# A decoder trunk on one core: the mixers' own products in float32r, and the modulation sums in other stages

## The chip, the cores and the metric

The kernel runs on one core of one Trainium2 chip. The metric is the device time of one execution in microseconds. Three runs of the kernel before gave 998.33, 993.95 and 998.08 us, a median of 998.08 us.

## The reference

Two residual layers work on 256 positions of 1024 channels. Each layer has three sub-layers: a half-step SwiGLU (inner width 2816), a mixer, and another half-step SwiGLU. Each is preceded by an RMSNorm with a shift and a scale, and followed by a gate; shift, scale and gate come from a conditioning vector c through a 1024 x 18432 product, two halves of which are the two layers' 9 x 1024.

```python
def modnorm(x, g, shift, scale):
    return rmsnorm(x, g) * (1 + scale[:, None, :]) + shift[:, None, :]
def swiglu(h, w_gate, w_up, w_down):
    return (jax.nn.silu(h @ w_gate) * (h @ w_up)) @ w_down
...
# even mixer: p = h @ w_in, split in u, q, k, v; the output is concat(pool(u), diff_attention(q, k, v)) @ w_out
#   pool, group g of 4, window w = 2, 4, 8, 16:
#     pooled = trailing mean over min(pos + 1, w) positions - u;  y = (pooled @ w_group[g]) * scale
#   diff_attention, 4 heads with two halves of 64 channels:
#     s = causal(q . k / 8);  p = softmax(s);  a = p[0] - lam * p[1];  o = rmsnorm(a @ v)
# odd mixer: mLSTM in two chunks of 128 positions; its decay matrices need rows of running maxima, one per head
```

All of it is in float32, the positions lie along the free dimension, the channels along the 128 partitions.

## The kernel before, in words

The work is one stream of 2560 weight tiles of 128 x 128, called units, in a fixed order: gate and up of the first feed-forward (352 units), down (176), the even mixer's input projection (128) and output projection (64), the second feed-forward (528), then layer 1 in the same way with an input projection of 192. A unit (`mm3`, L338) is three float32r matmuls with 256 columns, with weight and activation each split into a high part rounded to float32r and the rest: wh x rh (L341), wl x rh (L342), wh x rl (L343).

Sixteen units are a chunk, one DMA of 1 MiB on SP's queue (L294) into a ring of five buffers `raw`. Half a chunk, eight units, is split by ScalarE (high half `wh`, L299) and VectorE (low half `wl`, L300), with four buffers for each; `split_to` runs two halves ahead of the unit that is issued (`look`). The modulation product runs beside this on VectorE: a modulation chunk, also 1 MiB on the same queue and in the same ring (L249), holds two columns, each of which is one multiply and sum of 128 x 1024 (L267, in `mod_sums`) with c. `MOD_POINTS` (L121) says how many of the 72 modulation chunks are read before which weight chunk, by straight lines between points; they are loaded in front of the weights of that chunk and summed behind its second low half. The columns are needed by `need_mod` in the sequence norm, gate, norm, and so on.

The order of the work around the stream is written out by hand. A piece of a mixer is a generator, a lane, which yields the number of units after which it continues; `tick` runs the lanes due at each unit, so their instructions stand between the matmuls of the stream in each engine's queue. If something is asked for before its lane has reached it, `run_until` steps all lanes at once.

At the start of a sub-layer the statistics of the norm are not yet there. The first pairs of blocks (`NEARLY`, 5) therefore multiply with the unnormalised x (`xh`, `xl`, 258 columns with the shift) and are scaled with `rext` on the way out of PSUM; meanwhile `stats_lane` makes the statistics (unit 15 and 22) and from then on normalises one of eight parts of x every four units (`norm_x`, L442, three operations on VectorE, ScalarE, VectorE), which the later blocks read as `xs`.

In the even mixer `head(h)` computes scores: for each half a product of an identity with a constant mask over 384 columns (L660), then q . k in fp32 with 64 rows, 128 and 256 columns (L662, L664), maximum on VectorE (L671), exponential on ScalarE (L675). `pool_group` multiplies u with w_pool (L730) and the result with a band matrix of 128 x 384 (L735 to L737), all in fp32. In the odd mixer `gates` broadcasts four rows of maxima to all partitions by an fp32 product (L842). The output projection takes its inner tiles in the order `EVEN_OUT_K`, for the first blocks all but the last ones first (`sweep`).

Of the kernel before, what the change touches and what calls it, by code (L numbers as in the profile page):

```python
# [38 lines left out]
EVEN_OUT_K = (4, 5, 6, 3, 2, 7, 1, 0)  # L39
# [3 lines left out]
NEARLY = 5  # L43
# [48 lines left out]
def weight_units():  # L92

    units = []
    for l in range(DEPTH):
        for s in range(2):
# [24 lines left out]
MOD_POINTS = ((8, 8), (41, 32), (72, 44), (104, 56), (124, 68), (145, 72))  # L121
# [15 lines left out]
def trunk_kernel(ctx: ExitStack, tc: tile.TileContext, xT, crow, pack, pack2, wst, mst, outT):  # L137
# [7 lines left out]
    hid = ctx.enter_context(tc.tile_pool(name="hid", bufs=46))  # L145
# [34 lines left out]
    masks3 = const.tile([P, 3 * P], F32R, name="masks3")  # L180
# [3 lines left out]
    band = const.tile([P, len(WINDOWS), 3 * P], F32, name="band")  # L184
# [23 lines left out]
    def constants():  # L208
        m3 = tmp.tile([P, 2, 3 * P], F32, tag="sc", name="m3")[:, 0, :]
        nc.gpsimd.memset(m3, 0.0)  # L210
        for i in (0, 2):
            nc.gpsimd.affine_select(out=m3[:, i * P:(i + 1) * P], in_=m3[:, i * P:(i + 1) * P], pattern=[[-1, P]],
                                    compare_op=ALU.is_ge, fill=NEG, base=0, channel_multiplier=1)
        nc.gpsimd.tensor_copy(masks3, m3)
# [7 lines left out]
        for g, w in enumerate(WINDOWS):  # L222
            nc.gpsimd.memset(band[:, g, :], 1.0 / w)
            for t in range(w - 1):
                nc.gpsimd.memset(band[:, g, t:t + 1], 1.0 / (t + 1))
            for lo, n in ((0, T), (T, P)):
                m = band[:, g, lo:lo + n]
                nc.gpsimd.affine_select(out=m, in_=m, pattern=[[1, n]], compare_op=ALU.is_ge, fill=0.0,
                                        base=0, channel_multiplier=-1)
                nc.gpsimd.affine_select(out=m, in_=m, pattern=[[-1, n]], compare_op=ALU.is_ge, fill=0.0,  # L230
                                        base=w - 1, channel_multiplier=1)
                nc.gpsimd.tensor_tensor(out=m[:, 0:P], in0=m[:, 0:P], in1=ident, op=ALU.subtract)
        nc.sync.dma_start(pk2, pack2)
        nc.gpsimd.tensor_copy(wgh, pcol("w_gates", 0, 64))
        nc.gpsimd.tensor_tensor(out=wgl, in0=pcol("w_gates", 0, 64), in1=wgh.bitcast(F32), op=ALU.subtract)

# [187 lines left out]
    def stats_lane(wait, key, then=None):  # L424
# [60 lines left out]
    def swiglu(f, hs, gate, bias_g, up, bias_u):  # L485

        sg = tmp.tile([P, T], F32, tag="sg", name=nm("sg"))
# [148 lines left out]
    def even_mixer(l, nxt):  # L636
# [17 lines left out]
        def head(h):  # L654
            yield 8
            q, kk = parts.pop(("q", h)), parts.pop(("k", h))
            pp = [one(), one()]
            for c in range(2):
                rows = slice(64 * c, 64 * c + 64)
                nc.tensor.matmul(pp[c][:, 0:3 * P], lhsT=identr, rhs=masks3, start=True, stop=False,  # L660
                                 skip_group_check=True)
                nc.tensor.matmul(pp[c][:, 0:P], lhsT=q[rows, 0:P], rhs=kk[rows, 0:P], start=False, stop=True,  # L662
                                 skip_group_check=True)
                nc.tensor.matmul(pp[c][:, P:3 * P], lhsT=q[rows, P:T], rhs=kk[rows, 0:T], start=False, stop=True,  # L664
                                 skip_group_check=True)
# [3 lines left out]
            for i in range(2):  # L669
                for c in range(2):  # L670
                    nc.vector.tensor_reduce(out=mx[:, i, c:c + 1], in_=pp[c][:, cols[i]], axis=AX.X, op=ALU.max)  # L671
            nc.vector.tensor_scalar(out=nb, in0=mx, scalar1=-0.125, scalar2=None, op0=ALU.mult)
            for i in range(2):
                for c in range(2):
                    nc.scalar.activation(sc[:, c, cols[i]], pp[c][:, cols[i]], AF.Exp, bias=nb[:, i, c:c + 1],  # L675
# [48 lines left out]
        def pool_group(g, src, bias):  # L724
            u = keep(src, bias)
            yield 16
            pz = one()
# [305 lines left out]
```

## Time and profile before

| | before |
|---|---|
| median of three runs | 998.08 us |
| profiled execution | 998.09 us |
| its span | 996.4 us |
| TensorE matmuls | 973.5 us busy, 98% |
| VectorE | 758.1 us, 76% |
| ScalarE | 528.0 us, 53% |
| GpSimd | 217.9 us, 22% |
| moved by DMA | 247.18 MB, 248 GB/s on average |

The span runs from the first to the last instruction of the profiled execution. Busy times of different engines overlap. A matmul's record is longer than the distance to the next one, because matmuls are pipelined, so the distance of two starts is its price in a stream. An fp32 matmul shows as two records. The stages of the first layer begin at about 17.7 (gate and up), 150.3 (down), 212.5 (input projection), 273.6 (output projection) and 301.7 us (second feed-forward); the odd mixer's input projection runs from 679.3 to 772.6 us.

### The profile page before, as it was taken

Reading aid. Unit: us, or ns where it says so; the run is one execution under the profiler, and the core shown is the slowest. Engines: PE = TensorE matmul, PEld = TensorE weight load, DVE = VectorE, ACT = ScalarE, POOL = GpSimd, SP = SyncE. Lnnn points to the kernel's source line nnn. Section 1 sums busy time; section 2 is a strip of 40 time slices with the busy share of each in tenths; the row PEclk is TensorE's granted clock in tenths of the full one; section 3 lists DMA queues with packets and bytes.
Section 4 is the critical chain, followed back from the end, with each engine's and each line's share of the span. In section 5 each row is a group of like instructions: output and inputs, shape, how many; then the busy total and the mean of one; then the engine's idle time right before and its main releaser. Section 6 shows DMA issues by size and latency. Waiting matters only on the chain.

```text
span 996.4 us, 19641 instructions
## 1 busy us (share of the span) xinstructions
PE 973.5 (98%) x8032; PEld 958.8 (96%) x8032; DVE 758.1 (76%) x1201; ACT 528.0 (53%) x872; POOL 217.9 (22%) x223
## 2 busy tenths in 40 slices
PE   7999999999999999999999999999999999999996
PEld 6899999999999999999999999999899999999996
DVE  5979998989879876777798676788867988555452
ACT  3475544448766544444465444445767655444441
POOL 4953220110112322211122222001010113222011
PEclk9999999999999999999999999999999999999998
DMA  9978888875846766766758766676565746565521
GB/s 341 317 295 318 328 329 319 341 284 206 298 155 246 271 245 254 277 252 235 290 182 291 288 245 248 269 293 258 200 223 185 280 171 244 205 229 175 187 105 43
DMA packets 36093, 247.18 MB, mean 248 GB/s; under 512 B 4001, under 2 KB 4385, under 8 KB 7458
## 3 DMA queue, kind: packets, MB, share of 16 engines
q1 hardware_dynamic: 35856, 245.81, 66.7%
q8 instruction: 63, 1.03, 0.4%
q14 instruction: 28, 0.23, 0.1%
q10 hardware_dynamic: 146, 0.11, 0.0%
HBM read 244.86 MB, written 1.05 MB: 247 GB/s over the span
## 4 chain that ended last, share of the span: by engine, by line
PE 82%; DVE 9%; ACT 3%; issue 3%; POOL 1%; DVEq 0%; ACTq 0%; POOLq 0%
PE one L343 26%; PE one L341 26%; PE one L342 26%; DVE wl L300 3%; DVE rawm L267 3%; ACT wh L299 1%; DVE xs L447 1%; POOL hr L401 1%; DVE xn L445 1%; PE one L418 0%; DVE xl L587 0%; DVE t L512 0%; DVE h L490 0%; ACT L488 0%; PE one L842 0%
## 5 line engine op out<-in xcount | busy, mean ns | idle before, releaser
L300 DVE TENSOR_TENSOR wl<-raww,wh 128x1024 fp32r<-128x1024 f32 x320 | 395.5, 1239 | 162.4 <-ACT wh L299 161.1
L299 ACT ACTIVATE wh<-raww 128x1024 fp32r<-128x1024 f32 x320 | 337.2, 1056 | 226.7 <-PE one L343 197.3
L341 PE MATMUL one<-xs,wh 128*128 128x256 f32 x976 | 275.3, 282 | 0.0
L342 PE MATMUL one<-xs,wl 128*128 128x256 f32 x976 | 272.9, 280 | 1.0 <-DVE wl L300 1.0
L343 PE MATMUL one<-xs,wh 128*128 128x256 f32 x976 | 273.1, 280 | 0.0
L341 PE MATMUL one<-hid,wh 128*128 128x256 f32 x832 | 233.7, 281 | 0.2 <-ACT hid L601 0.2
L343 PE MATMUL one<-hid,wh 128*128 128x256 f32 x832 | 233.7, 281 | 0.0
L342 PE MATMUL one<-hid,wl 128*128 128x256 f32 x832 | 233.3, 280 | 0.0
L342 PE MATMUL one<-xh,wl 128*128 128x258 f32 (+1 forms) x752 | 207.5, 285 | 3.2 <-DVE wl L300 2.9
L341 PE MATMUL one<-xh,wh 128*128 128x258 f32 (+1 forms) x752 | 208.1, 287 | 1.8 <-ACT xh L585 1.8
L343 PE MATMUL one<-xl,wh 128*128 128x258 f32 (+1 forms) x752 | 204.6, 283 | 0.0
L493 POOL TENSOR_TENSOR hid<-h,hid 128x256 fp32r<-128x256 f32 x88 | 123.3, 1402 | 340.1 <-ACT hid L492 340.1
L342 PEld LDWEIGHTS one<-xs,wl 128*128 128x128 f32 x976 | 183.6, 188 | 1.4 <-DVE wl L300 1.2
L341 PEld LDWEIGHTS one<-xs,wh 128*128 128x128 f32 x976 | 183.0, 187 | 1.2 <-issue 1.0
L343 PEld LDWEIGHTS one<-xs,wh 128*128 128x128 f32 x976 | 183.1, 188 | 0.0
L341 PEld LDWEIGHTS one<-hid,wh 128*128 128x128 f32 x832 | 156.8, 188 | 0.4 <-ACT hid L601 0.4
L343 PEld LDWEIGHTS one<-hid,wh 128*128 128x128 f32 x832 | 156.6, 188 | 0.2 <-DVE hid L602 0.2
L342 PEld LDWEIGHTS one<-hid,wl 128*128 128x128 f32 x832 | 156.7, 188 | 0.0
L267 DVE CUSTOM_DVE_ANT_0 rawm<-rawm,cact,pk 128x1024 f32<-128x1024 f32 x112 | 150.5, 1371 | 0.0
L342 PEld LDWEIGHTS one<-xh,wl 128*128 128x128 f32 x752 | 140.6, 191 | 5.4 <-DVE wl L300 5.2
L341 PEld LDWEIGHTS one<-xh,wh 128*128 128x128 f32 x752 | 140.3, 191 | 4.1 <-ACT xh L585 2.3
L343 PEld LDWEIGHTS one<-xl,wh 128*128 128x128 f32 x752 | 138.8, 189 | 0.2 <-DVE xl L587 0.2
(222 smaller groups left out, 727.0 us busy)
## 6 DMA issues: line engine op xcount, KB each, us to landing
raww<-wst SPq DMA_DIRECT2D x152, 1024.0 KB, 4.8
rawm<-mst SPq DMA_DIRECT2D x71, 1024.0 KB, 4.9
raww<-wst SPq DMA_DIRECT2D x16, 512.0 KB, 6.4
xa<-xT SPq DMA_DIRECT2D x2, 512.0 KB, 4.7
rawm<-mst SPq DMA_DIRECT2D x2, 512.0 KB, 7.4
outT<-fin SPq DMA_DIRECT2D x3, 256.0 KB, 2.8
pk<-pack SPq DMA_DIRECT2D x1, 416.0 KB, 6.9
outT<-fin SPq DMA_DIRECT2D x2, 128.0 KB, 2.3
```

What stands on the lines that cost most here:

```text
L267: nc.vector.tensor_tensor_reduce(out=ri, in0=ri, in1=cact, scale=factor, scalar=first, op0=ALU.mult, op1=ALU.add, accum_out=modc[n // KT][ ...
L299: nc.scalar.activation(whs[i], src, AF.Copy)
L300: ins = nc.vector.tensor_tensor(out=wls[i], in0=src, in1=whs[i].bitcast(F32), op=ALU.subtract)
L341: nc.tensor.matmul(out, lhsT=wh, rhs=rh, start=start, stop=False, skip_group_check=skip)
L342: nc.tensor.matmul(out, lhsT=wl, rhs=rh, start=False, stop=False, skip_group_check=skip)
L343: nc.tensor.matmul(out, lhsT=wh, rhs=rl, start=False, stop=stop, skip_group_check=skip)
L401: nc.gpsimd.tensor_tensor(out=r, in0=v, in1=mhalf[:, 0:width], op=ALU.pow)
L445: nc.vector.scalar_tensor_tensor(out=xn, in0=x[k], scalar=a, in1=r, op0=ALU.mult, op1=ALU.mult)
L447: nc.vector.scalar_tensor_tensor(out=to[1], in0=xn, scalar=b, in1=to[0].bitcast(F32), op0=ALU.add, op1=ALU.subtract)
L493: nc.gpsimd.tensor_tensor(out=hl[:, 0:T], in0=h, in1=hh[:, 0:T].bitcast(F32), op=ALU.subtract)
```

## The change

The even mixer's q and k are kept as high and low float32r parts, and the scores are three float32r products per block of scores, with the two row halves in alternation; the mask is added on VectorE in one operation with the maximum, and the exponential reads the result from SBUF. Pooling is done on VectorE by shifted sums, in front of w_pool, which is then three float32r products. The row broadcast of the odd mixer uses two float32r products in place of one fp32 product. `MOD_POINTS` has other points. x is normalised every 7 units, with six early pairs. The even output projection has another order of inner tiles and another sweep. The lanes' yields of `head` and `pool_group` are other ones.

```diff
-EVEN_OUT_K = (4, 5, 6, 3, 2, 7, 1, 0)
+EVEN_OUT_K = (4, 5, 3, 6, 2, 1, 0, 7)
+PAD = 16
-NEARLY = 5
+NEARLY = 6
-                units += [(("out_even", l // 2), k, n) for n, k in sweep(range(KT), EVEN_OUT_K, 3, 2)]
+                units += [(("out_even", l // 2), k, n) for n, k in sweep(range(KT), EVEN_OUT_K, 4, 4)]
-MOD_POINTS = ((8, 8), (41, 32), (72, 44), (104, 56), (124, 68), (145, 72))
+MOD_POINTS = ((8, 8), (20, 18), (33, 31), (45, 32), (78, 47), (111, 68), (145, 72))
-    hid = ctx.enter_context(tc.tile_pool(name="hid", bufs=46))
+    hid = ctx.enter_context(tc.tile_pool(name="hid", bufs=44))
...
         for k in range(KT):
-            yield 4
+            yield 7
             norm_x(k, rext[:, 0:T], A_cols[key][:, k:k + 1], shift[:, k:k + 1], xs[k])
...
         def head(h):
-            yield 8
+            yield 10
             q, kk = parts.pop(("q", h)), parts.pop(("k", h))
             pp = [one(), one()]
-            for c in range(2):
-                rows = slice(64 * c, 64 * c + 64)
-                nc.tensor.matmul(pp[c][:, 0:3 * P], lhsT=identr, rhs=masks3, start=True, stop=False,
-                                 skip_group_check=True)
-                nc.tensor.matmul(pp[c][:, 0:P], lhsT=q[rows, 0:P], rhs=kk[rows, 0:P], start=False, stop=True,
-                                 skip_group_check=True)
-                nc.tensor.matmul(pp[c][:, P:3 * P], lhsT=q[rows, P:T], rhs=kk[rows, 0:T], start=False, stop=True,
-                                 skip_group_check=True)
+            for to, qs, ks in ((slice(0, P), slice(0, P), slice(0, P)), (slice(P, 3 * P), slice(P, T), slice(0, T))):
+                for j, (a, b) in enumerate(((0, 0), (1, 0), (0, 1))):
+                    for c in range(2):
+                        rows = slice(64 * c, 64 * c + 64)
+                        nc.tensor.matmul(pp[c][:, to], lhsT=q[a][rows, qs], rhs=kk[b][rows, ks], start=j == 0,
+                                         stop=j == 2, skip_group_check=True)
...
-                    nc.vector.tensor_reduce(out=mx[:, i, c:c + 1], in_=pp[c][:, cols[i]], axis=AX.X, op=ALU.max)
+                    nc.vector.tensor_tensor_reduce(
+                        out=sc[:, c, cols[i]], in0=pp[c][:, cols[i]], in1=masks3[:, cols[i]], scale=1.0, scalar=NEG,
+                        op0=ALU.add, op1=ALU.max, accum_out=mx[:, i, c:c + 1])
...
         def pool_group(g, src, bias):
-            u = keep(src, bias)
-            yield 16
...
+            w = WINDOWS[g]
+            u = tmp.tile([P, PAD + T], F32, tag="sg", name=nm("pu"))
+            nc.vector.memset(u[:, 0:PAD], 0.0)
+            nc.scalar.activation(u[:, PAD:PAD + T], src, AF.Identity, bias=bias)
+            s, d = u, 1
+            while d < w:
+                n = tmp.tile([P, PAD + T], F32, tag="ps", name=nm("ps"))
+                lo = 2 * d - 1
+                nc.vector.tensor_tensor(out=n[:, lo:PAD + T], in0=s[:, lo:PAD + T], in1=s[:, lo - d:PAD + T - d],
+                                        op=ALU.add)
+                s, d = n, 2 * d
...
+            yield 22
             ps = one()
-            nc.tensor.matmul(ps[:, 0:P], lhsT=z[:, 0:P], rhs=band[:, g, 0:P], start=True, stop=True)
-            nc.tensor.matmul(ps[:, P:T], lhsT=z[:, 0:P], rhs=band[:, g, P:T], start=True, stop=False)
-            nc.tensor.matmul(ps[:, P:T], lhsT=z[:, P:T], rhs=band[:, g, T:3 * P], start=False, stop=True)
+            sl = slice(g * P, (g + 1) * P)
+            for j, (a, b) in enumerate(((wph, zh), (wpl, zh), (wph, zl))):
+                nc.tensor.matmul(ps[:, 0:T], lhsT=a[:, sl], rhs=b[:, 0:T], start=j == 0, stop=j == 2)
...
+            ph, pl = slot(F32R), slot(F32R)
+            nc.scalar.activation(ph[:, 0:T], src, AF.Identity, bias=bias)
+            nc.vector.scalar_tensor_tensor(out=pl[:, 0:T], in0=src, scalar=bias, in1=ph[:, 0:T].bitcast(F32),
+                                           op0=ALU.add, op1=ALU.subtract)
+            parts[blk] = (ph, pl)
...
             for h in range(NH):
                 pb4 = one()
-                nc.tensor.matmul(pb4[:, 0:T], lhsT=ident[0:4, h:h + 1].broadcast_to([4, P]), rhs=mr,
-                                 start=True, stop=True)
+                for j in range(2):
+                    nc.tensor.matmul(pb4[:, 0:T], lhsT=identr[0:4, h:h + 1].broadcast_to([4, P]), rhs=mrs[j],
+                                     start=j == 0, stop=j == 1)
```

In the part of `pool_group` left out, VectorE forms the mean minus the token (one operation over all positions, two short ones for the first w - 1), and z is split into a high part on ScalarE and a low part on VectorE. The `band` constants, 4 x 128 x 384, are no longer made on GpSimd; w_pool is split there into two float32r tiles.

## Rows read from the trace of the kernel before

**Rows 1.** The page, busy us, share of the span and instructions of each engine.
```profile
PE 973.5 (98%) x8032; PEld 958.8 (96%) x8032; DVE 758.1 (76%) x1201; ACT 528.0 (53%) x872; POOL 217.9 (22%) x223
```

**Rows 2.** Windows: length, busy us by engine, then clock, DMA share, GB/s.
```profile
74.00:150.30 76.30, 76.30 (x647) 76.30 (x646) 70.73 (x98) 39.91 (x60) 22.13 (x18) 1.00 0.85 324
150.30:212.50 62.20, 62.20 (x530) 62.20 (x529) 54.63 (x82) 29.22 (x38) 6.17 (x7) 1.00 0.84 320
160.00:170.00 10.00, 10.00 (x87) 10.00 (x86) 9.47 (x19) 4.75 (x8) 0.87 (x1) 1.00 0.96 381
212.50:273.60 61.10, 60.53 (x486) 57.07 (x485) 55.34 (x118) 44.60 (x114) 6.48 (x5) 1.00 0.71 257
```

**Rows 3.** Timeline of TensorE: start, us, instruction, count; 24 matmuls between the two starts.
```profile
688.53 0.28 PE L772 MATMUL one<-xh,wgh 128*8 128x258 f32 x1
...
691.37 0.28 PE L341 MATMUL one<-xh,wh 128*128 128x258 f32 x1
```

**Rows 4.** Timeline of TensorE: the score groups of two heads.
```profile
233.45 0.52 PE L660 MATMUL one<-masks,identr 128*128 128x384 f32 x2
233.90 0.50 PE L662 MATMUL one<-hid,hid 64*128 64x128 f32 x4
234.22 0.61 PE L664 MATMUL one<-hid,hid 64*128 64x256 f32 x4
234.76 0.39 PE L341 MATMUL one<-xh,wh 128*128 128x258 f32 x1
...
257.08 0.34 PE L660 MATMUL one<-masks,identr 128*128 128x384 f32 x1
257.35 0.49 PE L662 MATMUL one<-hid,hid 64*128 64x128 f32 x2
257.67 0.59 PE L664 MATMUL one<-hid,hid 64*128 64x256 f32 x2
...
259.41 0.39 PE L341 MATMUL one<-xs,wh 128*128 128x256 f32 x1
```

**Rows 5.** Timeline of TensorE: pooling of two groups each.
```profile
275.45 0.39 PE L735 MATMUL one<-band,hid 128*128 128x128 f32 x2
...
276.79 1.06 PE L730 MATMUL one<-pk,hid 128*128 128x128 f32 x8
277.61 0.36 PE L341 MATMUL one<-hid,wh 128*128 128x256 f32 x1
```

**Rows 6.** Timeline of TensorE: one row broadcast.
```profile
715.51 0.69 PE L842 MATMUL one<-mr,ident 4*128 4x256 f32 x2
716.14 0.39 PE L341 MATMUL one<-xh,wh 128*128 128x258 f32 x1
```

**Rows 7.** Waits of TensorE: us in total, times, longest.
```profile
PE one L342 <- DVE wl L300: 3.9, 8, 1.3
...
PE one L868 <- DVE hid L866: 1.7, 1, 1.7
...
PE one L710 <- ACT hid L705: 0.6, 1, 0.6
PE one L827 <- DVE dg L822: 0.4, 1, 0.4
PE one L808 <- DVE col L804: 0.3, 1, 0.3
```

**Rows 8.** Timeline of TensorE: a wait in the second feed-forward.
```profile
332.71 0.38 PE L342 MATMUL one<-xs,wl 128*128 128x256 f32 x1 [1.00 <-DVE wl L300]
```

**Rows 9.** VectorE by line, 150.3 to 212.5: busy us, mean ns, idle before.
```profile
L300 DVE TENSOR_TENSOR wl<-raww,wh 128x1024 fp32r<-128x1024 f32 x23 | 27.9, 1218 | 7.0 <-ACT wh L299 6.9
L267 DVE CUSTOM_DVE_ANT_0 rawm<-rawm,cact,pk 128x1024 f32<-128x1024 f32 x17 | 21.2, 1277 | 0.0
```

**Rows 10.** VectorE by line, 212.5 to 273.6 us, the even input projection.
```profile
L267 DVE CUSTOM_DVE_ANT_0 rawm<-rawm,cact,pk 128x1024 f32<-128x1024 f32 x12 | 15.1, 1275 | 0.0
...
L671 DVE TENSOR_REDUCE mx<-one 128x1 f32<-128x128 f32 (+1 forms) x16 | 4.8, 351 | 0.5 <-PE one L664 0.4
```

More of the change, by code (lines that the diff above doesn't have):

```diff
@@ L183, in trunk_kernel @@
     tri = const.tile([P, P], F32, name="tri")
-    band = const.tile([P, len(WINDOWS), 3 * P], F32, name="band")
+    icnt = const.tile([P, PAD], F32, name="icnt")
+    wph = const.tile([P, 512], F32R, name="wph")
+    wpl = const.tile([P, 512], F32R, name="wpl")
     wgh = const.tile([P, 64], F32R, name="wgh")
@@ L221, in constants @@
                                 fill=0.0, base=0, channel_multiplier=-1)
[L222 to L232, printed above, removed]
+        for t in range(PAD):
+            nc.gpsimd.memset(icnt[:, t:t + 1], 1.0 / (t + 1))
         nc.sync.dma_start(pk2, pack2)
@@ L235, in constants @@
         nc.gpsimd.tensor_tensor(out=wgl, in0=pcol("w_gates", 0, 64), in1=wgh.bitcast(F32), op=ALU.subtract)
+        nc.gpsimd.tensor_copy(wph, pcol("w_pool", 0, 512))
+        nc.gpsimd.tensor_tensor(out=wpl, in0=pcol("w_pool", 0, 512), in1=wph.bitcast(F32), op=ALU.subtract)
     mod_sched = mod_schedule(nchunks)
@@ L724, in pool_group @@
         def pool_group(g, src, bias):
-            u = keep(src, bias)
-            yield 16
-            pz = one()
-            for i in range(2):
-                sl = slice(i * P, (i + 1) * P)
-                nc.tensor.matmul(pz[:, sl], lhsT=u[:, sl], rhs=pcol("w_pool", g * P, P), start=True, stop=True)
-            z = slot()
-            nc.scalar.activation(z[:, 0:T], pz[:, 0:T], AF.Copy)
-            yield 18
+            w = WINDOWS[g]
[9 more added lines that the diff above has]
+                s, d = n, 2 * d
+            z = slot()
+            nc.vector.scalar_tensor_tensor(out=z[:, 0:T], in0=s[:, PAD:PAD + T], scalar=1.0 / w,
+                                           in1=u[:, PAD:PAD + T], op0=ALU.mult, op1=ALU.subtract)
+            e = z[:, 0:w - 1]
+            nc.vector.tensor_tensor(out=e, in0=s[:, PAD:PAD + w - 1], in1=icnt[:, 0:w - 1], op=ALU.mult)
+            nc.vector.tensor_tensor(out=e, in0=e, in1=u[:, PAD:PAD + w - 1], op=ALU.subtract)
+            zh, zl = slot(F32R), slot(F32R)
+            nc.scalar.activation(zh[:, 0:T], z[:, 0:T], AF.Copy)
+            nc.vector.tensor_tensor(out=zl[:, 0:T], in0=z[:, 0:T], in1=zh[:, 0:T].bitcast(F32), op=ALU.subtract)
+            yield 22
             ps = one()
-            nc.tensor.matmul(ps[:, 0:P], lhsT=z[:, 0:P], rhs=band[:, g, 0:P], start=True, stop=True)
-            nc.tensor.matmul(ps[:, P:T], lhsT=z[:, 0:P], rhs=band[:, g, P:T], start=True, stop=False)
-            nc.tensor.matmul(ps[:, P:T], lhsT=z[:, P:T], rhs=band[:, g, T:3 * P], start=False, stop=True)
+            sl = slice(g * P, (g + 1) * P)
+            for j, (a, b) in enumerate(((wph, zh), (wpl, zh), (wph, zl))):
+                nc.tensor.matmul(ps[:, 0:T], lhsT=a[:, sl], rhs=b[:, 0:T], start=j == 0, stop=j == 2)
             ys[g] = split_y(ps[:, 0:T], pcol("pool_scale", g))
```

21 lines of the change are left out of this document (12 added, 9 removed).

## The prediction

> **What bounds the kernel now.** The first view is the share of busy time by engine: TensorE's matmul row is at 98%, the next engine, VectorE, far below it [rows 1]. The reader then looks at the windows by stage: in the down projection of the first feed-forward (150.3 to 212.5 us) TensorE is busy for the whole stretch, at a granted clock of 1.00, the upper level of 2.4 GHz [rows 2]. So the kernel is one stream of matmuls; what takes time is (a) matmuls that stand in that stream beside the 7680 of the weights, (b) the places where TensorE waits. The price of one matmul of the stream is the distance of two starts, not the duration in the record: 24 float32r matmuls with 258 columns (lines 772 to 774, eight each) take 691.37 - 688.53 = 2.84 us, 0.118 us each [rows 3], and 7680 of those are 906 us of the span of 996.4. The third view is TensorE's waits [rows 7]: few and short. Outside the first 75 us two hold up the weights' own matmuls (1.0 and 1.3 us, both for a low half from VectorE, [rows 7, 8]), and the rest stand in the mixers.
>
> **Score products.** Today a head issues a mask product over 384 columns for each of its two halves and four fp32 products on 64 rows, each of which shows as two records. Four heads; the trace has two kinds of group. Where one half follows the other, the head takes 259.41 - 257.08 = 2.33 us; where the planner put the halves side by side it takes 234.76 - 233.45 = 1.31 us [rows 4]. Two heads are of each kind: 2 x (2.33 + 1.31) = 7.3 us. The same rows show a gift: four records of the 128-column product on both row halves last 234.22 - 233.90 = 0.32 us, and two records on one row half last 257.67 - 257.35 = 0.32 us too. Two products on different row halves cost what one costs. The new code issues 12 float32r products per head with the halves alternating, so I count six pairs. Three have 256 columns: 0.118 us each. Three have 128 columns, which no float32r row shows: at least half of 0.118, 0.06 us; at most the fp32 price, 0.32. I take one of fp32's two records, 0.16, the nearest row. Each change between 128 and 64 rows I put at 0.1 us: the two mask products, 1.5 times 256 columns each, would be 0.35 at the stream's pace and 0.45 passes (233.90 - 233.45). Before 2.33 us holds four changes, after there are two. So 3 x 0.118 + 3 x 0.16 + 0.2 = 1.03 us, 4.1 for four heads: **3.2 us less**. Lowest: 0.54 us a head, 5.1 less. Highest: no pairing and 0.32 for each narrow product, 6 x (0.118 + 0.32) + 0.2 = 2.83 us a head, 4.0 more.
>
> **Pooling.** Two groups' band products take 276.79 - 275.45 = 1.34 us and two groups' w_pool products 277.61 - 276.79 = 0.82 [rows 5]; four groups, 4.3 us. In their place stand 12 products of 256 columns in the form of the stream, 12 x 0.118 = 1.4. **2.9 us less**; the form is known, so within 0.3.
>
> **Row broadcast.** Four fp32 products of 716.14 - 715.51 = 0.63 us [rows 6] become eight of 0.118: 2.5 to 0.9. They contract over 4 rows only; if each head pays two changes of 0.1 it is 0.8 less, otherwise 1.6. I take **1.4**.
>
> **Waits.** x is normalised over 8 x 7 = 56 units and not 32, starting 22 units into the stage; with six early pairs (96 units) nothing needs it before unit 96, and the last part is issued at unit 78. A unit is 3 x 0.118 = 0.36 us, so VectorE gets 24 units, 8.6 us, more for the same work; those units bring three more low halves of 1.22 us. That leaves 4.9 us against waits of 1.0 and 1.3: both go, 2.3 us. The sixth pair adds two multiplications with rext per feed-forward, some 0.8 us, within that. The mixers' waits are L868 1.7, L710 0.6, L827 0.4, L808 0.3 [rows 7]. VectorE loses the modulation sums in front of them: in the even mixer 12 records, 15.1 us [rows 10]; by the schedule's points, seven chunks fall to one between chunks 33 and 45, and seven to one in the odd input projection (111 to 123). But L710 and L868 stand behind chains over ScalarE and GpSimd that stay, so I count half of the 3.0: 1.5. **3.8 us together**, bounds 0 and 5.3.
>
> **What this costs.** (1) The sums go to the stages in front. By chunk 33, 31 chunks are read and not 26: two more in 74 to 150.3, three in 150.3 to 212.5. A chunk is two records of 1.28 us. In the second stretch that is 7.7 us, beside 54.6 us of busy time in 62.2 [rows 2], 62.3 in all: exactly full. It is hidden if VectorE may run behind, and it may: it spent 7.0 us of this stretch waiting for ScalarE's high halves [rows 9], and those waits come from the four buffers (TensorE frees them), so it is up to two halves, 5.7 us, ahead of TensorE. I add the new records to VectorE's queue of this trace in order, and compare the end of each low half with the first matmul that uses it: the lead falls from 4 to 6 us to 3 to 5 and never to zero. If that cover were not there, 12.8 us (five chunks) would show. What is late is the last column of x at the start of the even mixer, behind some 1.7 us of queue where it had 1.5 us to spare: 0.2 us, at most 2. (2) SP's queue carries the same number of transfers in all, five of them earlier, each ahead of the weights of its chunk, in the same ring of five buffers. 150.3 to 212.5 has to move 19.9 MB + 3.1 MB, 371 GB/s; 160 to 170 moved 381 at a DMA share of 0.96 [rows 2]. So it fits, barely: 0.
> By the Trainium skill it would not: "DMA: Bandwidth & Descriptors", Specifications, gives some 358 GB/s as one core's limit from HBM, by which an estimate for these 23.0 MB is 64.4 us in place of 62.2, 2.2 us more. The 381 GB/s of this trace is above that limit, and "HBM Reference", Specifications, says the limit holds with both cores of a pair streaming; only one runs here.
> (3) In the first feed-forward of layer 1 (chunks 78 to 100) there are 14 chunks in place of 8; that stage has no wait today, and its normalising is spread too: 0. (4) In the mixers VectorE gets eight low halves of q and k, each behind ScalarE's high half (queued behind such a wait: the low halves of the weights), the mask in the maximum (16 records, 0.35 us today [rows 10], some 0.5 with an elementwise output), and about 9 us of shifted sums. Together some 18 us where 15.1 us of sums left. TensorE does not see it as long as the weights' low halves stay ahead. The pooling burst comes in the last 32 units, when z is due 22 units, 7.9 us, after its block; VectorE's chain for the widest group is some 4 us. (5) The output order puts head 3 last, so nothing is asked for before its lane has ended; pool group 0 is due at unit 24 and ready at about 25: 0.3 us. GpSimd loses the band constants and gains two splits of w_pool, off the path. The rest at nothing: 44 slots of hid hold the 22 x 2 halves of a feed-forward exactly, and the exponentials read SBUF on a ScalarE that is busy for 44.6 of 61.1 us [rows 2]. I book **1.0 us** for (1) and (5), bounds 0 to 4.
>
> **The sum** is made against the profiled execution, span 996.4 us and 998.1 us in all, equal to the median of 998.08. 998.1 - 3.2 - 2.9 - 1.4 - 3.8 + 1.0 = 987.8, rounded to **988 us**. Own range with the terms' bounds taken together where they are independent: 983 to 993.
>
> **Rivals.**
> Work only: TensorE's 7.5 us go, but the waits stay or come back elsewhere, since VectorE has 18 us of new work in the mixers and its queue waits for ScalarE eight times more. For: the mixers' VectorE time hardly falls. Against: the feed-forward waits have nothing to do with it. 998.1 - 7.5 = 990.6, with 1 us of new waits 991.6. Chance 0.15.
> Everything: scores at their lowest (5.1) and all waits of [rows 7] but those of the start (5.3): 998.1 - 5.1 - 2.9 - 1.6 - 5.3 + 0.3 = 983.5. For: the pairing is in the rows. Chance 0.10.
> Transfers: 150.3 to 212.5 us becomes bound by what lands, if it gets no more than midway between the 324 GB/s of the stretch before it and the 381 of its best ten [rows 2], 352: 23.0 MB take 65.4 us, 3.2 us more, 991. Against: the 381 were reached with the same ring. Chance 0.05.
> The narrow products do not get cheaper: pairing is lost and 128 columns cost the fp32 price, 4.0 more where I have 3.2 less: 988 + 7.2 = 995. The change then does not do what it says for its largest part. Against: one record of the fp32 form already lasts half of that. Chance 0.06.
> Slower: the first feed-forward is bound by VectorE. Place: 74 to 212.5 us; price: all five chunks, 12.8 us, since VectorE was at 70.7 of 76.3 us in its first part [rows 2]. It decides from 10.3 us on, that is when less than 2.5 of the 12.8 us are hidden: 987.8 + 12.8 = 1000.6. Against: the 7.0 us of [rows 9] alone are more than 2.5. Chance 0.06.
>
> **How the numbers follow.** 0.58 is left for 988. 982 to 995 leaves out the slower case, a part of the lowest, and the far ends of the first: some 0.2. A difference of 0.5%, 5 us, is what a measurement of this kernel can tell from none: faster means under 993.1. The narrow-products case and about 0.04 of the main case fall within; slower is the last rival alone. So 0.84, 0.10 and 0.06.
>
> **What would show it.** Score groups of about 1 us, and two starts of a pair a few ns apart; pooling as three starts 0.118 us apart; no wait for a low half behind the start; in 150.3 to 212.5 VectorE busy for nearly all of it with TensorE still unbroken, and DMA near 370 GB/s. It is wrong if TensorE waits for low halves there, if the narrow products take 0.2 us or more apiece, or if new waits of the mixers add up to more than 4 us.

## The result and the profile after

The changed kernel takes 1011.49 us (median of four runs, 1010.48 to 1012.57) against 998.13: a ratio of 1.0144, 95% interval 1.0115 to 1.0173. It is slower; 988 us was predicted, and the time lies far outside 982 to 995. Of the fifty runs of the kernel before that all comparisons below used, eight lie between 993.9 and 994.6 us and the others between 997.4 and 998.7, at the same granted clock, for a reason that is not known. The profiled execution took 1012.57 us, span 1010.8. Lines have moved: the stream is now lines 336 to 338 (was 341 to 343), the high and low halves 294 and 295 (299 and 300), the scores 657, a head's scaled output 700 and its transposition 705 (705 and 710), the pooling 723 to 745, the broadcast 860.

The page's busy line of after [rows 1]: TensorE's share falls from 98% to 97% although it has 20 matmuls fewer.

```profile
PE 978.1 (97%) x8012; PEld 964.9 (95%) x8012; DVE 776.8 (77%) x1267; ACT 526.5 (52%) x872; POOL 187.0 (19%) x186
```

The windows of after, at the stages of [rows 2]: length, busy us (count) of PE, PEld, DVE, ACT, POOL, clock, DMA share, GB/s.

```profile
74.00:150.30 76.30, 75.81 (x640) 75.58 (x639) 68.80 (x107) 36.63 (x58) 19.01 (x17) 1.00 0.89 330
150.80:218.20 67.40, 63.87 (x531) 62.73 (x530) 63.40 (x94) 29.59 (x40) 8.32 (x7) 1.00 0.91 341
160.00:170.00 10.00, 9.68 (x82) 9.47 (x81) 8.66 (x12) 5.54 (x8) 0.63 (x1) 1.00 0.96 372
218.20:283.80 65.60, 58.78 (x490) 56.57 (x489) 57.42 (x159) 47.13 (x117) 4.72 (x5) 0.96 0.52 192
```

The first down projection went from 62.2 to 67.4 us and is no longer unbroken; the even input projection from 61.1 to 65.6, with TensorE idle for 6.8 us of it. TensorE's waits of after [rows 7] name the two places:

```profile
PE one L337 <- DVE wl L295: 7.1, 12, 0.9
PE one L705 <- ACT hid L700: 6.1, 1, 6.1
...
PE one L886 <- DVE hid L884: 2.1, 1, 2.1
...
PE one L822 <- DVE col L818: 1.0, 1, 1.0
...
PE one L657 <- DVE hid L759: 0.5, 2, 0.3
```

What the edits were to remove is gone. TensorE's timeline of after shows scores, one broadcast and one pooling group, as [rows 4 to 6] did:

```profile
231.34 0.44 PE L657 MATMUL one<-hid,hid 64*128 64x128 f32 x4
232.11 0.73 PE L657 MATMUL one<-hid,hid 64*128 64x128 f32 x8 [0.34 <-DVE hid L759]
232.77 0.39 PE L336 MATMUL one<-xh,wh 128*128 128x258 f32 x1
...
250.99 0.95 PE L657 MATMUL one<-hid,hid 64*128 64x128 f32 x12
251.88 0.39 PE L336 MATMUL one<-xh,wh 128*128 128x258 f32 x1
...
286.88 0.28 PE L745 MATMUL one<-hid,wph 128*128 128x256 f32 x1
...
287.24 0.28 PE L336 MATMUL one<-hid,wh 128*128 128x256 f32 x1
...
727.67 0.38 PE L860 MATMUL one<-mrh,identr 4*128 4x256 f32 x1
727.89 0.28 PE L860 MATMUL one<-mrl,identr 4*128 4x256 f32 x1
728.10 0.39 PE L336 MATMUL one<-xh,wh 128*128 128x258 f32 x1
```

An undisturbed head takes 251.88 - 250.99 = 0.89 us (two do; the others 1.43 and 1.28, with 0.34 and 0.18 of waits for k's low half), together 4.5 against 7.3. A pooling group takes 0.36, four of them 1.44 against 4.3. A broadcast takes 0.43 against 0.63.

The stages of all kernels, in us, each from the start of its first weight matmul to that of the next stage's, worked out from the traces. GU1 and DN1: first gate-and-up and down; EVEN, ODD: the mixers' two projections; GU2-4: the other three gate-and-up stages.

```
                       GU1    DN1   EVEN   GU2-4    ODD    span
before               132.7   62.2   89.2   380.3  116.0   996.4
after                133.0   67.4   91.3   384.9  117.7  1010.8
e1  old points       132.3   62.2   97.4   382.8  116.2  1006.4
e2  weights first    132.3   64.5   95.4   384.9  116.1  1009.8
e3  pad 64           133.0   67.3   91.5   369.5  115.4   992.7
e4  split on GpSimd  133.0   67.3   92.7   384.9  116.2  1010.9
e5  before, pad 128  132.7   62.2   88.9   369.3  115.5   984.6
e6  pad 128          133.0   67.4   91.2   381.7  117.5  1007.4
e7  fp32 pooling     134.0   67.3   86.4   369.5  116.7   989.4
e8  sums on GpSimd   133.0   67.4   89.6   369.5  117.0   991.8
e9  e7 + old points  133.2   62.2   91.0   367.4  115.6   985.3
e10 e5 + new points  133.5   67.3   89.5   369.0  116.2   991.3
e11 half modulation  132.9   62.2   93.0   376.2  115.4   995.7
e12 e7 + between     133.9   62.2   87.4   369.5  116.6   985.3
e13 e7 + late        133.2   62.2   88.2   369.7  115.6   984.4
```

Between before and after the 14.4 us of span are DN1 +5.2, GU2-4 +4.6, EVEN +2.1, ODD +1.7, GU1 and the other down stages +0.8. ODD's share is mostly the clock: behind the wait of 2.1 us at L886 the granted clock is 0.60 over 764 to 768 us, and 22 matmuls start there; e4 has the same wait, a clock of 1.00 in that window, 35 starts, and an ODD of 116.2. Three causes were left to be told apart: the points, the wait at the end of the even input projection, and a slower stream in GU2-4.

### The profile page after: what moved, and what is told of

Its sections match the earlier page's. It is cut to its first block, busy times and chain, and to the rows that moved or that the text cites. A ratio compares the mean times of both kernels' runs of the same rounds, so it can differ in the third digit from the quotient of the medians.

```text
span 1010.8 us, 19650 instructions
## 1 busy us (share of the span) xinstructions
PE 978.1 (97%) x8012; PEld 964.9 (95%) x8012; DVE 776.8 (77%) x1267; ACT 526.5 (52%) x872; POOL 187.0 (19%) x186
## 4 chain that ended last, share of the span: by engine, by line
PE 65%; DVE 21%; ACT 6%; issue 5%; POOL 1%; DVEq 0%; ACTq 0%; POOLq 0%
PE one L336 21%; PE one L337 21%; PE one L338 21%; DVE wl L295 8%; DVE rawm L262 7%; ACT wh L294 3%; DVE xs L442 1%; DVE xn L440 1%; DVE h L485 1%; DVE t L507 0%; PE one L413 0%; POOL hid L488 0%; ACT hid L487 0%; ACT sc L670 0%; DVE xl L582 0%
## 5 line engine op out<-in xcount | busy, mean ns | idle before, releaser
L336 PE MATMUL one<-xs,wh 128*128 128x256 f32 x896 | 256.4, 286 | 0.0
L337 PE MATMUL one<-xs,wl 128*128 128x256 f32 x896 | 254.3, 284 | 1.6 <-DVE wl L295 1.6
L338 PE MATMUL one<-xs,wh 128*128 128x256 f32 x896 | 254.1, 284 | 0.0
L336 PE MATMUL one<-xh,wh 128*128 128x258 f32 (+1 forms) x832 | 231.0, 287 | 2.1 <-ACT xh L580 2.1
L337 PE MATMUL one<-xh,wl 128*128 128x258 f32 (+1 forms) x832 | 230.1, 284 | 2.0 <-DVE wl L295 1.9
L338 PE MATMUL one<-xl,wh 128*128 128x258 f32 (+1 forms) x832 | 226.8, 283 | 0.0
L337 PEld LDWEIGHTS one<-xs,wl 128*128 128x128 f32 x896 | 172.5, 193 | 2.1 <-DVE wl L295 2.0
L336 PEld LDWEIGHTS one<-xs,wh 128*128 128x128 f32 x896 | 172.5, 193 | 0.4
L338 PEld LDWEIGHTS one<-xs,wh 128*128 128x128 f32 x896 | 172.5, 192 | 0.0
L337 PEld LDWEIGHTS one<-xh,wl 128*128 128x128 f32 x832 | 156.1, 191 | 3.8 <-DVE wl L295 3.4
L336 PEld LDWEIGHTS one<-xh,wh 128*128 128x128 f32 x832 | 155.5, 191 | 3.6 <-ACT xh L580 2.6
L338 PEld LDWEIGHTS one<-xl,wh 128*128 128x128 f32 x832 | 153.9, 189 | 0.2 <-DVE xl L582 0.2
```

Of the source, the lines that this page charges most:

```text
L336: nc.tensor.matmul(out, lhsT=wh, rhs=rh, start=start, stop=False, skip_group_check=skip)
L337: nc.tensor.matmul(out, lhsT=wl, rhs=rh, start=False, stop=False, skip_group_check=skip)
L338: nc.tensor.matmul(out, lhsT=wh, rhs=rl, start=False, stop=stop, skip_group_check=skip)
```

## Experiments

### The modulation points

ScalarE's waits in the first down stage, before and then after (us in total, times, longest), had pointed to a change of the binding wait from TensorE to a transfer:

```profile
ACT wh L299 <- PE one L343: 24.1, 15, 1.8
```

```profile
ACT wh L294 <- DMA raww<-wst: 12.0, 8, 3.3
```

**e1**, the change with the points of before:

```diff
-MOD_POINTS = ((8, 8), (20, 18), (33, 31), (45, 32), (78, 47), (111, 68), (145, 72))
+MOD_POINTS = ((8, 8), (41, 32), (72, 44), (104, 56), (124, 68), (145, 72))
```

> The changed kernel with the schedule of modulation chunks of before; all else as changed. Theory (the front stage can't take five more chunks through its ring): the down projection of the first feed-forward goes back from 67.4 to about 62.2 us with no wait for a low half, and the wait of 0.9 us in the first feed-forward of layer 1 goes; the sums return to the mixers, where VectorE is then fuller, so the wait at the end of the even input projection (6.1 us) stays or grows by up to 3 us. Sum: 1011.5 - 5.2 - 0.9 + 0 to 3 = 1005 to 1008 us. Rival (the down projection is longer because of something else in the change, such as the memory layout or the longer normalising): that stage stays at 67 us, 1011 us.

1007.57 us (1.0096, 1.0079 to 1.0113). DN1 is back at 62.2, but the even mixer pays more than the change did: the wait for the heads' output grows to 10.3 us, by 4.2 where at most 3 was expected.

```profile
PE one L705 <- ACT hid L700: 10.3, 3, 8.2
```

**e2**, in the ring the weight chunk goes ahead of the modulation chunks due with it:

```diff
-                while mod_done[0] < mod_sched[c]:
-                    mod_chunk()
                 raws[c] = raw_pool.tile(...)
                 nc.sync.dma_start(raws[c], wst[c])
                 loaded[0] = c + 1
+                while mod_done[0] < mod_sched[c]:
+                    mod_chunk()
```

> The changed kernel, but a weight chunk is read ahead of the modulation chunks that go with it, not behind them; VectorE's work, the bytes and the ring of five buffers stay. Theory (ring order): today a weight chunk reuses the buffer of the modulation chunk two chunks back, whose sums end last, and lands some 5.5 us later; read first, it reuses the buffer of one three chunks back and is issued a chunk earlier. The 12 us of ScalarE waiting for weights in 150.8 to 218.2 us fall under 3, the stage goes from 67.4 to 62.2 to 63 us, and the time to about 1006. Rival one (DMA bandwidth: 22.9 MB there, 90% of the engines' time): the stage stays above 65 us, 1010. Rival two (VectorE simply has too much to do: 63.4 us busy): the same, but with ScalarE no longer waiting for weights while TensorE still waits for low halves.

1010.93 us (1.0130, 1.0115 to 1.0145). DN1 falls by 2.9 of its 5.2 us, less than forecast. The rate did not change: 22.0 MB land in the 64.5 us and 23.0 MB in the 67.4 of after, 341 GB/s in both, so the other order only moves one chunk (1 MB, 2.9 us at that rate) out of the stage. The total was missed because EVEN took 4.0 us more: at its start TensorE waits 1.4 us for the norm's statistics, and the granted clock is 0.58 over 222 to 226 us.

**e10** is the reverse of e1: before, with the padding of e5 (below), and the new points alone.

```diff
-MOD_POINTS = ((8, 8), (41, 32), (72, 44), (104, 56), (124, 68), (145, 72))
+MOD_POINTS = ((8, 8), (20, 18), (33, 31), (45, 32), (78, 47), (111, 68), (145, 72))
```

> The kernel before with 128 bytes of padding (986.46 us) and the new modulation points alone. Theory (the points alone delay the first down stage): that stage goes from 62.2 to 66.5 to 68 us with seven or so waits for the low halves, the even mixer loses nothing, total 990 to 993 us. Rival (the stage was slowed by other edits as well, or the even mixer wins as much from its lighter VectorE): stage under 64 us or total 985 to 988 us.

994.73 us (0.9970, 0.9956 to 0.9984; its five runs spread from 992.9 to 996.7), above the 990 to 993 of the theory. Against e5 DN1 goes from 62.2 to 67.3, all that it lost in the change and within the forecast for the stage; EVEN does not gain. The points alone cost this stage 5 us.

**e11**, with e3's padding, tells the landing of the transfers from VectorE's sums; it leaves out half of the modulation, so only this stage is read:

```diff
-        for i in range(parts):
-            nc.sync.dma_start(r[:, i * w:(i + 1) * w], mst[m][:, i * w:(i + 1) * w])
+        for i in range(max(1, parts // 2)):
+            n = min(w, D)
+            nc.sync.dma_start(r[:, i * w:i * w + n], mst[m][:, i * w:i * w + n])
...
-                ri = r[:, i * D:(i + 1) * D]
+                ri = r[:, 0:D]
```

> The change with 64 bytes of padding, where only the first half of each modulation chunk is loaded and both sums read that half (the second half of the modulation is left out); the sums, their order and the buffers are unchanged. Read in the first down stage alone. Theory (the landing of the transfers binds there): 512 KB less for each chunk, the stage goes from 67.3 back to 62.2 to 63 us and the waits for the low halves go. Rival (VectorE's sums and the freeing of the ring's buffers bind): the stage stays at 66 us or more.

997.46 us, one run. The first down stage by windows, of e10 and then of e11:

```profile
150.80:218.20 67.40, 63.91 (x531) 62.75 (x530) 62.94 (x91) 30.23 (x41) 8.46 (x8) 1.00 0.90 341
```

```profile
150.80:213.00 62.20, 62.20 (x530) 62.20 (x529) 61.19 (x92) 28.17 (x38) 7.24 (x7) 1.00 0.81 286
```

With as many sums on VectorE (22 in the stage in both), and VectorE busy for 61.2 of 62.2 us, TensorE is unbroken again; one wait of 1.0 us for VectorE's part of x follows in EVEN. So the sums alone do not hold the stage up. The rates fit a limit on what lands: the eight kernels whose DN1 got longer (after, e2, e3, e4, e6, e7, e8, e10) all move 340 to 342 GB/s in it, while the stages that stay unbroken need less (before and e1 320, e13 334, e12 338). What sets the 341 is not shown. SP's queue, which issues the transfers, waits for nearly all of the stage for VectorE to free a buffer of the ring, in before (56.6 of 62.2 us) as in after (59.4 of 67.4; its largest part is shown below), so the size of the ring and the speed of the transfers are not told apart, and no run kept the bytes with fewer sums. ScalarE's wait for transfers is no measure of it either: in e11 it is 20.3 us.

```profile
SPq L289 <- DVE wl L295: 36.4, 11, 4.4
```

### The wait at the end of the even input projection

The timeline of after, all engines, around the 6.1 us:

```profile
275.16 0.42 ACT L739 ACTIVATE hid<-hid 128x256 fp32r<-128x256 f32 x1 [1.06 <-DVE hid L737]
...
278.42 0.42 ACT L739 ACTIVATE hid<-hid 128x256 fp32r<-128x256 f32 x1 [1.35 <-DVE hid L737]
...
279.00 0.27 ACT L696 ACTIVATE hid<-one 128x128 f32<-128x128 f32 x1
...
280.47 0.16 DVE L394 TENSOR_SCALAR hv<-ss 128x2 f32<-128x2 f32 x1
...
280.70 0.81 POOL L396 TENSOR_TENSOR hr<-hv,mhalf 128x2 f32<-128x2 f32 x1 [17.02 <-DVE hv L394]
...
281.55 0.62 ACT L700 ACTIVATE hid<-one,hr 128x128 f32<-128x128 f32 x2 [1.93 <-POOL hr L396]
...
281.97 0.73 PE L705 MATMUL one<-ident,hid 128*128 128x128 f32 x2 [6.09 <-ACT hid L700]
```

Read it backwards. Head 2's output goes through ScalarE's squares (L696), VectorE (L394), GpSimd (L396) and ScalarE again (L700). The squares stand in ScalarE's queue behind L739, the high half of a pooling result, which waits for VectorE's shifted sums; L394 stands behind those sums in VectorE's. The windows around it show what follows:

```profile
274.00:276.00 2.00, 1.88 (x16) 1.68 (x14) 1.96 (x9) 0.94 (x4) 0.00 (x0) 1.00 0.36 66
276.00:282.00 6.00, 0.03 (x1) 0.03 (x1) 5.16 (x15) 2.73 (x10) 0.81 (x1) 0.76 0.48 183
282.00:286.00 4.00, 4.00 (x19) 3.93 (x20) 2.05 (x6) 2.15 (x6) 0.00 (x0) 0.51 0.51 217
286.00:290.00 4.00, 4.00 (x36) 4.00 (x35) 1.67 (x3) 2.19 (x7) 0.00 (x0) 1.00 0.01 4
```

After TensorE stood for 6 us the granted clock is 0.51, the lower level (1.2 GHz), for 4 us more: 19 matmuls start where 36 do in the next 4 us. That is about 2 us on top of the 6.1.

**e4**, the split of the pooled result on GpSimd (both instructions, in place of ScalarE and VectorE):

```diff
-            nc.scalar.activation(zh[:, 0:T], z[:, 0:T], AF.Copy)
-            nc.vector.tensor_tensor(out=zl[:, 0:T], ...)
+            nc.gpsimd.tensor_copy(zh[:, 0:T], z[:, 0:T])
+            nc.gpsimd.tensor_tensor(out=zl[:, 0:T], ...)
```

> The changed kernel with the split of the pooled z (high and low part) on GpSimd and not on ScalarE and VectorE. Theory (head of line): the 6.1 us wait of TensorE at 276 us is for head 2's rows, whose two squares stand in ScalarE's queue behind a pooling group's high half, which waits for VectorE's shifted sums, and whose statistics then stand in VectorE's queue behind the next group. Without the pooling's ScalarE and VectorE halves the wait falls to under 3 us, TensorE's clock does not drop behind it, and in all 4 to 7 us go: 1005 to 1007 us. Rival (VectorE's sums alone make the queue): the wait stays above 5 us, 1011 us. Rival two: GpSimd's halves come too late and the wait moves to the output projection, 1011 us.

1012.64 us (1.0148, 1.0133 to 1.0163). The wait stays, 6.8 us: to free ScalarE of L739 is not enough while VectorE carries the sums.

**e8**, the ten sums on GpSimd, the rest in a later step:

```diff
-                nc.vector.tensor_tensor(out=n[:, lo:PAD + T], ...)
+                nc.gpsimd.tensor_tensor(out=n[:, lo:PAD + T], ...)
...
+            yield 12
             z = slot()
...
-            yield 22
+            yield 10
```

> The change with 64 bytes of padding, the ten shifted sums on GpSimd instead of VectorE, and what follows them (scaling, the first columns, the split) issued 12 units later, 10 units ahead of the matmuls. Theory: some 4 us leave VectorE's queue and ScalarE no longer waits for them, the wait for the head's output falls under 2 us: total 985 to 990 us. Rival (GpSimd takes over a microsecond for each sum, and the pooled results are late themselves): a wait of 4 us or more for a pooled result, total 992 to 998 us.

993.91 us (0.9975, 0.9956 to 0.9993). **e7**, the pooling of before in the changed kernel (band and w_pool products in float32), with padding that gives the placement of e3:

```diff
-            u = tmp.tile([P, PAD + T], F32, tag="sg", name=nm("pu"))
...
-            for j, (a, b) in enumerate(((wph, zh), (wpl, zh), (wph, zl))):
-                nc.tensor.matmul(ps[:, 0:T], lhsT=a[:, sl], rhs=b[:, 0:T], start=j == 0, stop=j == 2)
+            u = keep(src, bias)
+            yield 16
...
+            nc.tensor.matmul(ps[:, 0:P], lhsT=z[:, 0:P], rhs=band[:, g, 0:P], start=True, stop=True)
...
```

> The change with the pooling of before (float32 matmuls with the projection and the band) in place of the shifted sums, and padded so that the spacing on normalised x is that of the kernel with 64 bytes of padding (994.78 us). Theory (the shifted sums fill VectorE and ScalarE's queue behind it, and head 2's output waits there): the wait of 6 to 7 us for the head's output goes, the clock stays at 2.4 GHz, TensorE gets 2.9 us of pooling back: total 987 to 990.5 us. Rival (VectorE is full there for other reasons, such as the masks and the splits of the scores): a wait of 3 us or more stays, total 993 to 998 us.

991.19 us (0.9937, 0.9917 to 0.9957). Twelve microseconds at the end of the projection, of e3 (the change's pooling), e8 and e7:

```profile
268.00:280.00 12.00, 7.50 (x63) 7.10 (x61) 11.23 (x28) 8.43 (x21) 0.00 (x0) 0.98 0.36 133
```

```profile
268.00:280.00 12.00, 9.31 (x76) 8.59 (x75) 7.17 (x16) 7.59 (x22) 7.48 (x11) 1.00 0.35 130
```

```profile
266.00:278.00 12.00, 11.68 (x102) 11.45 (x101) 5.92 (x19) 8.71 (x27) 0.69 (x1) 1.00 0.44 156
```

VectorE is busy for 11.2, 7.2 and 5.9 of 12 us, and TensorE for 7.5, 9.3 and 11.7. In e7 the wait is gone, and EVEN is 5.0 us shorter than in e3 though TensorE has the 2.9 us of pooling back: wait and low clock cost 7.9 us for a gain of 2.9. Its total still misses the forecast of 987 to 990.5 by 0.7 us: GU1 is 1.0 and ODD 1.3 us longer than in e3, the latter with 3.4 us at the lower clock from 747.9 us on. e8 missed its forecast and fell in its rival's range: a wait of 2.4 us for the head's output stays and 1.6 us for the halves of the result (lines 597 and 598) come, where the rival had 4 us or more.

### The spacing of the matmuls

One count had no place in the prediction. In the last gate-and-up stage (840 to 900 us), where TensorE never waits and the clock is 1.00 in both kernels, before issues 512 matmuls and after 503, in the same form but for the first 4.8 us of after, which are still on the unnormalised x:

```profile
840.00:900.00 60.00, 60.00 (x512) 60.00 (x511) 37.60 (x44) 28.48 (x42) 15.59 (x11) 1.00 0.61 221
```

```profile
840.00:900.00 60.00, 60.00 (x503) 60.00 (x501) 34.70 (x40) 28.88 (x44) 15.63 (x11) 1.00 0.59 209
```

The normalised x (xs) lies at the same address in both; the weight halves moved by 1984 bytes per partition, since constants in front of them changed. **e3** and **e6** put an unused tile of 64 and of 128 bytes ahead of the weight buffers of the change, **e5** one of 128 bytes into the kernel before:

```diff
     wgl = const.tile([P, 64], F32R, name="wgl")
+    pad = const.tile([P, 16], F32, name="pad")
```

> The changed kernel with 64 unused bytes per partition behind the constants, which shifts the weight buffers and all that follows by 64 bytes; the normalised x stays. Theory (address phase): in the changed kernel the starts of the split weights and of the normalised x are equal modulo 128 (96 and 96), before they were not (32 and 96), and matmuls on normalised x come every 120 ns and not every 118. With the shift they come every 118 ns again: 2688 matmuls x 2.2 ns = 5.9 us, 1005.6 us. Rival (the pace comes from data, DMA or clock): it stays at 120 ns and 1011.5 us.

> The change with an unused constant tile of 128 bytes per partition in place of 64. Theory: the spacing is a function of the distance between the two addresses modulo 256 (0 bytes 120 ns, 64 bytes 114 ns, 192 bytes 118 ns so far); at 128 bytes it comes out between 112 and 118 ns, total 993 to 1005 us. Rival (modulo 128 alone decides, as 0 and 128 are alike): 120 ns again, total 1010 to 1013 us.

> The kernel before with an unused constant tile of 128 bytes per partition, so that the weight halves and the normalised x stand to each other in SBUF as in the padded kernel of the change (weight halves 64 bytes behind the rows of x, counted modulo 256). Theory (the start address of the moving rows against that of the weights sets the spacing of the matmuls): spacing on normalised x falls from 118 ns to 114 ns here too, the three gate-and-up stages lose 4 to 5 us each, total 982 to 987 us. Rival (the 114 ns came with another part of the change, such as the later normalisation): spacing stays 118 ns, total 997 to 999 us.

e3: 994.78 us (0.9969, 0.9957 to 0.9981). e6: 1009.98 (1.0129, 1.0108 to 1.0150). e5: 986.46 (0.9893, 0.9871 to 0.9915). The same window of e3, e6 and e5:

```profile
840.00:900.00 60.00, 60.00 (x531) 60.00 (x531) 36.98 (x42) 29.93 (x44) 15.79 (x12) 1.00 0.61 217
```

```profile
840.00:900.00 60.00, 60.00 (x508) 60.00 (x507) 34.02 (x39) 28.80 (x43) 15.15 (x11) 1.00 0.58 209
```

```profile
840.00:900.00 60.00, 60.00 (x532) 60.00 (x532) 37.05 (x42) 29.95 (x44) 15.68 (x11) 1.00 0.63 230
```

The distance is the address of the weight halves less that of xs, modulo 256 bytes, worked out from the order and sizes of the kernels' tiles, since no trace shows an address. It goes with the median spacing of starts on xs in GU2 to GU4 so: 0 bytes (after) 120 ns; 64 bytes (e3, e5) 113 to 114; 128 (e6) 119; 192 (before) 118. e3 expected 118 and got more; e6's own theory (112 to 118 ns) failed, and its rival's total came to pass, but with another pattern (starts 115 to 122 ns apart, where after has 120 nearly always). That it is a distance and not the weights' own address shows in GU1: its rows of x lie 32 bytes further on for each k (the inner tile), so all eight distances in steps of 32 occur in one stage, and the mean spacing behind the first product is the same for one distance within 2 ns in before, after, e3, e5 and e6 (0 bytes: 116 to 117; 32: 116 to 117; 160: 119; 224: 122 to 124). It is not the same as in GU2 to GU4, though, where 0 bytes give 120; so the distance is part of the rule and not all of it.

### What is left at equal placement

e3 against e5 is the change against before at one distance: 8.1 us of span more. **e9** keeps the change's scores, broadcast, output order and late normalisation, with the pooling and the points of before (the diffs of e7 and e1 together); **e12** and **e13** start from e9 and move the points:

```diff
-MOD_POINTS = ((8, 8), (41, 32), (72, 44), (104, 56), (124, 68), (145, 72))
+MOD_POINTS = ((8, 8), (20, 18), (33, 28), (45, 32), (78, 47), (111, 68), (145, 72))    # e12
+MOD_POINTS = ((8, 8), (33, 27), (45, 32), (72, 44), (104, 56), (124, 68), (145, 72))   # e13
```

> The change with the pooling of before, the modulation points of before and 128 bytes of padding: what is left of the change is the float32r scores and row broadcast, the other output order and the normalisation every 7 units. Theory (three separate causes that add): from the kernel with the pooling of before (991.19 us) the first down stage gives back 5 us, the short waits in the two gate-and-up stages 1.5 us, the start of the program and the odd mixer some 1 to 2 us: total 980 to 984 us, below the padded kernel before (986.46 us). Rival (the sums that return to the even mixer and to the second half make it wait there instead): total 985 to 989 us.

> The kernel with the pooling of before and 128 bytes of padding, with points between the two sets: 18 chunks by weight chunk 20 as in the change, then 28 instead of 31 by chunk 33, so that the first down stage carries 10 chunks instead of 13 and the even mixer 3 to 4 instead of 6 with the points of before. Theory (each stage pays for the chunks put into it): the first down stage stays at 62.2 to 63 us, the even mixer's input comes out between 59 and 62 us (63.4 with the points of before), total 981.5 to 985 us. Rival (the down stage has no room for even one chunk more than before): stage 65 us or more, total 986 to 989 us.

> The kernel with the pooling of before and 128 bytes of padding, with the points of before except in the two stages around the even mixer: 27 chunks by weight chunk 33, 32 by chunk 45 and 44 by chunk 72 (before: 26, 33 and 44). Theory (the sums cost only where they collide, and the rest of the change gives 2 to 5 us at equal placement): first down stage 62.2 us, even mixer's input 59 to 60.5 us, gate-and-up stages 122.5 us without waits, odd mixer 92.9 us: total 981 to 984.5 us, below the padded kernel before (986.46 us). Rival (what the float32r forms take from TensorE comes back as waits for the heads' results wherever the sums are put): total 985 to 988 us.

986.00 us (0.9882, 0.9867 to 0.9897), 987.01 (0.9886, 0.9870 to 0.9903) and 986.09 (0.9893, 0.9876 to 0.9911). All three beat both kernels and tie with e5, the kernel before with 128 unused bytes. The total of each fell in its rival's range, but not always in the rival's way. In e9 it did: EVEN is 2.0 us longer than in e5, with 2.2 us of waits for heads' outputs (0.6 in e5) and 3.4 us at the lower clock from 263.5 us on. In e12 and e13, DN1 (62.2) and the even input projection (59.3 and 60.6) came out about as expected. In e13 EVEN's waits for heads' outputs and for the halves of q and k add up to 2.2 us against 0.6 in e5, and GU2 takes 124.75 us against 122.45 in e9, with waits of 0.8 us for the norm's statistics and 0.7 for a low half. In e12 the loss lies in GU1, GU2, GU3 and ODD, 0.7 to 1.2 us each against e9, ODD's with a clock of 0.59 over 744 to 748 us. A small part is a price of the late normalisation at this distance: in GU2-4 products on the unnormalised x come every 120 ns (median) in every kernel and those on xs every 113 here, and the sixth early pair turns 48 of the second kind into the first in each stage; GU3, without waits in both, takes 122.2 us in e5 and 122.5 in e9.

## Why the prediction was wrong

**The steps that were right.** Scores: 0.89 us for an undisturbed head (1.03 predicted), 2.8 less in all with the waits (3.2 predicted). Pooling: 2.9 less, as predicted. Broadcast: 0.8 less, the bound for two changes of pace, not the 1.4 taken. The work left TensorE's stream; 6.5 us instead of 7.5.

**Step (2) of the costs failed first.** It took 371 GB/s as "it fits, barely: 0" from ten microseconds at 381. After moved 341 over the stage, though the same ten microseconds show 372: a mean over a stage with bursts and gaps is no peak. The rival "transfers" had this mechanism, and the midway 352 was still too high: 67.4 us, not 65.4. By the Trainium skill's page "DMA: Bandwidth & Descriptors", Specifications, the estimate was 64.4 us (23.0 MB over 358 GB/s are 64.2); its sign was right, and the trace stays below that figure over the stage (341) while single stretches exceed it (372 over ten microseconds). It is no full account: the eight kernels that lost in DN1 stop at 340 to 342.

**Step (1) failed with it.** The 7.0 us of [rows 9] were room for VectorE as long as ScalarE's high halves waited for TensorE. That was true of before; in after they waited for transfers, 12.0 us, and the room was gone (VectorE's wait for them fell from 6.9 to 2.0 us). Adding the new records to VectorE's queue kept every landing time of the old trace, which is what changed. The slower rival had the down stage right and its cause wrong, or at most half right: in e11 VectorE has all the sums and TensorE does not wait.

**Step (4) failed at the even mixer.** "TensorE does not see it as long as the weights' low halves stay ahead": they did, and TensorE waited 6.1 us all the same, for a head's output that passes through the same two queues. The 4 us chain of the widest group was compared with its own 7.9 us of slack, and not with who stands behind it on ScalarE and VectorE. The wait then cost some 2 us of low clock, a term that the sum did not have. Of the prediction's three signs of being wrong two came: waits for low halves in the down stage (3.5 us, five times) and new waits of the mixers above 4 us.

**Waits, and a term that was missing.** The 1.3 us of the last gate-and-up went, the 1.0 of the first became 0.7 and 0.9 came in the next (gone in e1 and e9 with the old points), and the odd mixer's rose (L886 2.1, L822 1.0, where [rows 7] have 1.7 and 0.3): little of the 3.8 was there. And the price of a matmul of the stream was taken from [rows 3] as fixed: 7680 x 0.118. Over all products of GU2-4 (gaps above 300 ns left out) the mean went from 118.5 to 120.2 ns; for 3 x 1056 of them that is 5.4 us, and with 0.7 us less of waits there it makes the 4.6. Under e3 it went down to 115: 15.4 of the 18.1 us of span that 64 bytes gave.

**The lesson in the sum.** The bounds of 0 to 4 us for all costs were drawn around two small steps, (1) and (5), while (2) and (4) stood at nothing with no upper end. At equal placement, e9, e12 and e13 show the predicted gain of the scores, the broadcast and the late normalisation as nil within the noise: at the three sets of points that were tried, new waits and low clock cost about what these edits give. Why e13's GU2 waits where before's points there cost e9 nothing was not tried.

## What to carry to other kernels

Before work is moved to a stage, ask of each wait in it what would end it next; slack that exists because a later engine is slow is gone when the transfer becomes the late one. Follow every in-order queue that a new chain enters and list who stands behind it, not only whether the chain itself is in time. And when the allocation of on-chip memory shifts, compare the spacing of unchanged matmuls in a stage without waits first: here that alone was worth more than the change.

## What was not expected of the hardware

The spacing of float32r matmuls of 256 columns went from 120 to 113 ns by the place of the weights against the moving rows, at a granted clock of 1.00 throughout. The Trainium skill, "TensorE: Matmul & The Clock Gate", Step-by-step: what each phase is for, says that the weight loads and the moving operand have read ports of their own, so that loading the next weights takes nothing from the running matmul; the five kernels above speak against taking the two as independent, since the spacing of the same matmuls goes by the distance between the two operands. What collides was not shown. Distance is also not the whole of it: beside GU1's other spacings, in e11, placed as e3, GU2 and GU3 ran at 118 ns and only GU4 at 113; this stays open.
